# Two seams of the gated MLP and the first loads of a two-layer decoder trunk, rearranged together

## The chip, the cores and the metric

The kernel runs on one core of one Trainium2 chip. The metric is the device time of one execution in microseconds (us), given as the median of three runs. All stretches below are counted from the start of the profiled span.

## The reference, cut to what matters

Two layers over 1024 positions of width 1024, in float32. The first has a differential attention and causal pooling beside each other, the second a sliding-window attention; each ends in the same gated MLP.

```python
def conv_glu_ffn(x, norm_g, w_up, conv_w, conv_b, w_down):
    S = x.shape[1]
    h = rms_norm(x, norm_g) @ w_up                      # 1024 -> 2 x 2816
    hp = jnp.pad(h, ((0, 0), (CONV_W - 1, 0), (0, 0)))
    c = conv_b
    for j in range(CONV_W):
        c = c + conv_w[j] * hp[:, j:j + S]
    gate, up = jnp.split(c, 2, axis=-1)
    return x + (jax.nn.silu(gate) * up) @ w_down        # 2816 -> 1024

def reference(x, ...):
    for layer in range(DEPTH):                          # DEPTH = 2
        x = diff_pool_layer(x, ...) if layer % 2 == 0 else swa_layer(x, ...)
        x = conv_glu_ffn(x, f_norm[layer], f_w_up[layer], ...)
    return x
```

## The kernel before, in words

Everything is held transposed: the model's width lies on the 128 partitions (eight tiles `x[d]`), the 1024 positions on the free axis, in two halves of 512 columns. Each float32 operand is split into a high part (ScalarE copy, L131) and a low part (VectorE subtraction, L132), and each product of two operands is three matmuls (high by high, high by low, low by high). The tile framework's scheduler fixes the order of each engine's instructions when the kernel is built, by priorities (`urgent`) and a model of time; on the chip each engine runs its list in that order and waits on semaphores. So a late instruction holds up all that stand behind it on its engine, or on its DMA queue.

In order of time the program does: loads, RMS norm and the pooling projections (`run`, `a_pools`, 0 to 53 us); mixer A (to 400); `ffn_up` of layer 0 (416 to 864); `ffn_down` of layer 0 (to about 1045); mixer C (to 1450); `ffn_up` and `ffn_down` of layer 1 (1452 to 2122).

**The beginning.** `run` issues everything on SyncE's queue: the parameters, then by turns two tiles of the first half of x (L997) and one 512 KB pooling weight `a_u[i]` (L152, `load_split`), which is split in one piece of 1024 columns. `a_pools` (L945) goes through d for two weights together.

**The start of ffn_up.** `scaled_feed` gets each finished tile of x (h is its half), squares it on ScalarE into an `hf` tile (a pool of four buffers) and sums the squares on VectorE; after the last, `norm_stats` transposes the sum on TensorE (L240), computes 1/sqrt on VectorE, broadcasts it with TensorE (L251), and VectorE scales the eight tiles (L341), which are split. The first three of 22 pairs of weight tiles are multiplied plainly (`plain`, L372): i = 0 and 1 on the first half, i = 0 and 1 on the second, then i = 2. Each product is 24 matmuls and ends in an evacuation by ScalarE (L411). The evacuated tiles go through the convolution (ScalarE L379, VectorE L380 and L382) and the gate (L388, L392). The rest is done by seven products per i; their operands are sums of weight tiles, VectorE L466.

**The start of ffn_down.** Seven products p = 1, 5, 6, 3, 7, 2, 4, each over K = 11 chunks k of 12 matmuls (L634). For product 1, chunk k needs a weight tile and the tile `b11[k]` of the gated activations, for product 5 the sums of two of each. `fetch` loads weights on SyncE's queue into a pool that `stages` names (L571, or L578 for two halves), FETCH chunks ahead; `gather` makes the sums LEAD chunks ahead (VectorE L592), `prepare` splits the operands AHEAD chunks ahead. The activations come back from DRAM (`gd`) on GpSimd's queue: `b1` (k below EARLY, four tiles), `b11` from k = 4 (L673), `b11` below 4 (L676), `b12` (L677), x (L680), `b22` (L682), `b21` (L684). The last gated tile is stored to `gd` shortly before.

Of the kernel before, what the change touches and what calls it, by code (L numbers as in the profile page):

```python
# [13 lines left out]
F32 = mybir.dt.float32  # L14
F32R = mybir.dt.float32r
I32 = mybir.dt.int32
AF = mybir.ActivationFunctionType
# [38 lines left out]
LO_OUT = 0  # L56
EARLY = 4
AHEAD = 3
LEAD = 8
FETCH = 14  # L60

PAR_NORM = 0
PAR_AQ, PAR_AK, PAR_SUB, PAR_CQ, PAR_CK = 32, 33, 34, 35, 36
# [5 lines left out]
class Trunk:  # L69
# [251 lines left out]
    def scaled_feed(self, x):  # L321
        nc = self.nc

        def after(d, h, xs):
            with self.urgent(8000):
                if d is not None:
                    nc.scalar.dma_start(self.nspill[d * P:(d + 1) * P, h * HALF:(h + 1) * HALF], xs)
                    sq = self.half()
                    nc.scalar.activation(sq[:], xs, AF.Square)
                    if d == 0:  # L330
                        self.nacc[h] = sq
                    else:
                        acc = self.nacc[h]
                        nc.vector.tensor_tensor(out=acc[:], in0=acc[:], in1=sq[:], op=ALU.add)
                    return
                self.norm_stats(h)
                sl = slice(h * HALF, (h + 1) * HALF)
                for k in range(ND):
                    g = self.par[:, PAR_NORM + 8 * self.nidx + k:PAR_NORM + 8 * self.nidx + k + 1]
                    xs = x[k][:, sl]  # L340
                    nc.vector.scalar_tensor_tensor(  # L341
                        out=xs, in0=xs, scalar=g, in1=self.nrbc[:, sl], op0=ALU.mult, op1=ALU.mult)
                    self.split2(xs, self.nxg[k][h])
        return after

    def ffn_up(self, layer, x, gd):
# [72 lines left out]
        plain(1, 0, 0, "s", "T")  # L419
        plain(1, 0, 1, "q", "T")  # L420
        raws[2] = load(2, ("wr", "wr"))
        plain(0, 1, 0, "s", "T")
        plain(0, 1, 1, "q", "T")
        weights(2)
        plain(1, 1, 0, "s", "T")
        plain(1, 1, 1, "q", "T")


        T1, T2, T3, T4 = [], [], [], []
# [117 lines left out]
    def ffn_down(self, layer, xs, gd, after, begin=lambda part: None):  # L547
# [7 lines left out]
        pairs = {1: (0, lo), 6: (0, lo), 3: (K, lo), 2: (K, lo), 4: (K, hi)}  # L555
        raws, parts, ops = {}, {}, {}
        stages = {p: ("r", "wr", "r", "wr", "r") for p in (5, 6, 3, 7, 2)}
        stages[1], stages[4] = ("wr", "wr", "x", "x", "x", "x"), ("r",)
        taken = dict.fromkeys(stages, 0)

        def stage(p):
# [33 lines left out]
        def operand(src):  # L595
            op = self.big("ws", F32R, HL)
            self.split2(src, op)
            return op
# [23 lines left out]
        def prepare(p, k):  # L622
            l, m = parts.pop((p, k))
            with self.urgent(12000):
                ops[p, k] = operand(l), operand(m)

        banks = {}

# [40 lines left out]

        for n in range(FETCH):  # L670
            fetch(*seq[n])
        for k in range(EARLY, K):
            nc.gpsimd.dma_start(b11[k], g(k, hi))  # L673
        for k in range(K):
            if k < EARLY:
                nc.gpsimd.dma_start(b11[k], g(k, hi))  # L676
            nc.gpsimd.dma_start(b12[k], g(k, lo))  # L677
        x = [self.big("x") for _ in range(ND)]
        for d in range(ND):
            nc.gpsimd.dma_start(x[d][:], xs[d * P:(d + 1) * P, :])  # L680
        for k in range(K):
            nc.gpsimd.dma_start(b22[k], g(K + k, lo))  # L682
        for k in range(K):
            nc.gpsimd.dma_start(b21[k], g(K + k, hi))  # L684
        for n in range(LEAD):
            gather(*seq[n])
        for n in range(AHEAD):
# [615 lines left out]
    def run(self):  # L1303
# [8 lines left out]
        self.nc.sync.dma_start(self.par[:], I["params"])  # L1312
        x = [self.big("x") for _ in range(ND)]
        w = []
        for i in range(4):
            self.load_half(I["xT"], x, 0, 2 * i, 2 * i + 2)
            w.append(self.load_split(I["a_u"][i], eng=self.nc.vector, stage="wr" if i < 2 else "t"))
        self.idn = self.pc.tile([P, P], F32, name="idn", tag="idn")
        self.nc.sync.dma_start(self.idn[:], I["ident"])
        self.load_half(I["xT"], x, 1, 0, ND)  # L1320
# [123 lines left out]
```

## Time and profile before

| | |
|---|---|
| median of 3 runs | 2121.87 us (2121.12 to 2127.75) |
| the profiled execution | 2124.41 us, its span 2122.2 us |
| TensorE busy | 2016.3 us (95%) in 10440 matmuls |
| VectorE, ScalarE, GpSimd busy | 1602.0 us (75%), 1107.2 us (52%), 257.8 us (12%) |
| the chain that ended last | TensorE 82%, VectorE 7%, ScalarE 4%, DMA 3% |
| mean granted clock of TensorE | 0.982 |

TensorE is the engine whose work fills the span; what is not its work is the time in which it stands idle and the stretches in which its granted clock is below 1. The page averages over stages with different limits, so the argument is made from single stretches. Besides TensorE's list of waits, the timelines of the two seams of each MLP and of the first 14 us are what is to be read.

### The profile page before, as it was taken

How to read it: one execution, taken by the hardware profiler on the slowest of the kernel's cores; microseconds unless marked ns; L12 is line 12 of the kernel's file. 1: busy time of each engine (PE TensorE's matmuls, PEld its weight loads, DVE VectorE, ACT ScalarE, POOL GpSimd, SP SyncE). 2: the span in 40 equal slices, each digit the busy share in tenths (PEclk: the TensorE clock that was granted, in tenths of full speed). 3: DMA queues.
4: the chain of work that ended last, by engine and by line, in shares of the span. 5: the costliest groups of instructions: out<-in, count | busy, mean ns of one | idle time of the engine just before them, and what ended most of it. 6: DMA issues, size and time to landing. Idle time of an engine off the chain costs nothing.

```text
span 2122.2 us, 28436 instructions
## 1 busy us (share of the span) xinstructions
PE 2016.3 (95%) x10440; PEld 1719.0 (81%) x10440; DVE 1602.0 (75%) x2882; ACT 1107.2 (52%) x2115; POOL 257.8 (12%) x449
## 2 busy tenths in 40 slices
PE   8999999889999999699999989999999999979999
PEld 6999877677888888588789988777788888867887
DVE  6677787877787777598863887777978777758975
ACT  5476755444455554345454875654645455433443
POOL 0322452000000002300013321200000000031000
PEclk9999999999999999899999999999999999999999
DMA  4210121302212224763431101212221222268342
GB/s 170 90 49 23 64 95 61 119 30 90 90 70 86 84 90 164 275 217 105 144 115 40 51 21 50 73 58 80 92 87 70 80 90 90 89 229 312 100 164 85
DMA packets 82333, 216.97 MB, mean 102 GB/s; under 512 B 9361, under 2 KB 9873, under 8 KB 82193
## 3 DMA queue, kind: packets, MB, share of 16 engines
q1 hardware_dynamic: 65296, 169.00, 23.0%
q0 software_dynamic: 9984, 33.56, 4.3%
q10 hardware_dynamic: 6912, 12.59, 1.6%
q8 instruction: 82, 1.34, 0.3%
q14 instruction: 59, 0.48, 0.1%
HBM read 173.17 MB, written 41.94 MB: 101 GB/s over the span
## 4 chain that ended last, share of the span: by engine, by line
PE 82%; DVE 7%; ACT 4%; DMA 3%; issue 2%; POOL 1%; SPq 0%; ACTq 0%; DVEq 0%; POOLq 0%
PE pss L372 22%; PE psq L372 12%; PE pss L634 7%; PE psq L634 6%; PE psd L720 6%; PE psd L123 5%; PE psd L372 5%; PE psd L634 4%; PE pss L720 3%; PE psq L123 2%; PE psq L893 1%; DMA b<-gd 1%; PE pss L945 1%; PE pss L791 1%; PE pss L792 1%
## 5 line engine op out<-in xcount | busy, mean ns | idle before, releaser
L372 PE MATMUL pss<-xg,ws 128*128 128x512 f32 x1248 | 297.0, 391 | 10.8 <-DVE xg L132 6.1
L372 PEld LDWEIGHTS pss<-xg,ws 128*128 128x128 f32 x1248 | 234.5, 189 | 62.3 <-DVE xg L132 7.0
L634 PE MATMUL pss<-ws,ws 128*128 128x512 f32 x726 | 209.5, 398 | 34.3 <-ACT ws L131 27.0
L372 PE MATMUL pss<-T,ws 128*128 128x512 f32 x912 | 224.6, 390 | 3.4 <-ACT ws L131 3.4
L372 PEld LDWEIGHTS pss<-T,ws 128*128 128x128 f32 x912 | 171.1, 188 | 39.6 <-ACT ws L131 4.2
L634 PEld LDWEIGHTS pss<-ws,ws 128*128 128x128 f32 x726 | 138.0, 192 | 66.1 <-ACT ws L131 27.9
L634 PE MATMUL psq<-ws,ws 128*128 128x512 f32 x660 | 191.5, 393 | 0.0
L720 PE MATMUL psd<-ws,xg 128*128 128x256 f32 x1344 | 184.0, 285 | 2.2 <-DVE hms L729 1.7
L720 PEld LDWEIGHTS psd<-ws,xg 128*128 128x128 f32 x1344 | 171.5, 191 | 4.7 <-DVE hms L729 2.3
L372 PE MATMUL psq<-xg,ws 128*128 128x512 f32 x696 | 168.5, 391 | 0.0
L132 DVE TENSOR_TENSOR ws<-hf,ws 128x512 fp32r<-128x512 f32 x160 | 109.6, 689 | 73.4 <-ACT ws L131 73.1
L372 PEld LDWEIGHTS psq<-xg,ws 128*128 128x128 f32 x696 | 131.1, 188 | 27.2
L131 ACT ACTIVATE ws<-wr 128x512 fp32r<-128x512 f32 (+1 forms) x156 | 114.2, 737 | 68.9 <-PE pss L372 23.7
L634 PEld LDWEIGHTS psq<-ws,ws 128*128 128x128 f32 x660 | 125.4, 190 | 26.4
L634 PE MATMUL psd<-ws,ws 128*128 128x512 f32 x462 | 145.6, 397 | 0.8 <-DVE ms L242 0.8
L123 PE MATMUL psd<-xg,ws 128*128 128x512 f32 x528 | 140.2, 404 | 3.1 <-DVE x L272 2.3
L131 ACT ACTIVATE ws<-hf 128x512 fp32r<-128x512 f32 x160 | 100.0, 630 | 76.1 <-PE psq L372 33.3
L677 POOL DMA_DIRECT2D xg<-gd x22 | 12.1, 552 | 988.8 <-PE pss L372 961.0
L132 POOL TENSOR_TENSOR ws<-wr,ws 128x1024 fp32r<-128x1024 f32 x38 | 95.0, 2506 | 284.8 <-ACT ws L131 242.3
L380 DVE SCALAR_TENSOR_TENSOR x<-x,conv,x 128x1023 f32<-128x1023 f32 x80 | 102.6, 1282 | 29.2 <-ACT x L379 28.9
L123 PEld LDWEIGHTS psd<-xg,ws 128*128 128x128 f32 x528 | 97.1, 192 | 23.2 <-DVE x L272 4.3
L372 PE MATMUL psq<-T,ws 128*128 128x512 f32 x456 | 115.6, 390 | 0.0
(263 smaller groups left out, 4071.1 us busy)
## 6 DMA issues: line engine op xcount, KB each, us to landing
wr<-in_dram SPq DMA_DIRECT2D x102, 512.0 KB, 3.5
x<-in_dram SPq DMA_DIRECT2D x44, 512.0 KB, 4.4
gd<-x SPq DMA_DIRECT2D x40, 512.0 KB, 2.6
r<-in_dram SPq DMA_DIRECT2D x64, 256.0 KB, 3.8
r<-in_dram SPq DMA_DIRECT2D x28, 512.0 KB, 3.8
xd<-x ACTq DMA_DIRECT2D x48, 256.0 KB, 2.2
xg<-gd POOLq DMA_DIRECT2D x44, 256.0 KB, 5.2
b<-gd POOLq DMA_DIRECT2D x44, 256.0 KB, 8.6
```

Source lines behind the costliest of these rows:

```text
L123: self.nc.tensor.matmul(out, a, b, start=(k == 0), stop=(k == n - 1))
L131: nc.scalar.activation(hi, raw, AF.Copy)
L132: (eng or nc.vector).tensor_tensor(out=lo, in0=raw, in1=hi.bitcast(F32), op=ALU.subtract)
L372: nc.tensor.matmul(bank[:], a, b, start=start and k == 0, stop=k == n - 1, skip_group_check=open)
L380: nc.vector.scalar_tensor_tensor(out=c[:, 1:], in0=hr[:, :S - 1], scalar=cw(1), in1=c[:, 1:], op0=ALU.mult, op1=ALU.add)
L634: nc.tensor.matmul(banks[p][m][:], l, r, start=opens and n == 0, stop=closes and n == 2, skip_group_check=p != 2)
L677: nc.gpsimd.dma_start(b12[k], g(k, lo))
L720: self.nc.tensor.matmul(out, a, m[:, d % 4, :], start=(n == 0), stop=(n == 23))
L791: nc.tensor.matmul(out, q[:, qs], his[m][:, ks], start=True, stop=False)
L792: nc.tensor.matmul(out, q[rows, qs], lo[rows, ks], start=False, stop=True)
L893: nc.tensor.matmul(po[:, :256], tt[:, kb * P:(kb + 1) * P], v, start=(b == 0 and t == 0), stop=(b == j and t == 1))
L945: nc.tensor.matmul(pu[:], a, b, start=d + n == 0, stop=d == ND - 1 and n == 2)
```

## The change

Three parts. `scaled_feed` squares the tiles of the second half into the pool `t` in place of `hf`, and the four second-half products of i = 0 and 1 run as four open banks, chunk by chunk, with their four evacuations behind them. In `ffn_down` the weights of product 1 are staged in `wr` alone and those of product 5 in `r, r, wr`; LEAD and FETCH are smaller; `b12` and eight `b22` are issued first, and `b11` below 4, x, the last three `b22` and `b21` are issued later: each such load is preceded by a one-column ScalarE copy into its tile out of the operand of a given chunk, so that it can't start before this chunk is prepared. At the beginning ScalarE's queue issues the first half of x, and the pooling weights are loaded and split by halves, two tensors by turns.

```diff
-LEAD = 8
-FETCH = 14
+LEAD = 5
+FETCH = 11
...
-                    sq = self.half()
+                    sq = self.half() if h == 0 else self.big("t", F32, (P, HALF))
...
-        plain(0, 1, 0, "s", "T")
-        plain(0, 1, 1, "q", "T")
+        four = [(i, k, self.bank(b)) for i in range(2) for k, b in ((0, "s"), (1, "q"))]
+        for kh in range(2):
+            for d in range(4):
+                for i, k, po in four:
...
+                    for n, (a, b) in enumerate(((ah, bh), (ah, bl), (al, bh))):
+                        nc.tensor.matmul(po[:], a, b, start=kh + d + n == 0, stop=kh * d * n == 6)
         weights(2)
-        plain(1, 1, 0, "s", "T")
-        plain(1, 1, 1, "q", "T")
+        for i, k, po in four:
+            nc.scalar.activation(hrs[i, k][:, h1], po[:], AF.Copy)
...
-        stages[1], stages[4] = ("wr", "wr", "x", "x", "x", "x"), ("r",)
+        stages[1], stages[5], stages[4] = ("wr",), ("r", "r", "wr"), ("r",)
...
                 ops[p, k] = operand(l), operand(m)
+            release(p, k)
...
+        x = [self.big("x") for _ in range(ND)]
+        asked = {}
+        def ask(dst, src, when):
+            asked.setdefault(when, []).append((dst, src))
+        def release(p, k):
+            for dst, src in asked.pop((p, k), ()):
+                nc.scalar.activation(dst[:, 0:1], ops[p, k][0][:, 0, 0:1].bitcast(F32), AF.Copy)
+                nc.gpsimd.dma_start(dst, src)
         for k in range(EARLY, K):
             nc.gpsimd.dma_start(b11[k], g(k, hi))
         for k in range(K):
-            if k < EARLY:
-                nc.gpsimd.dma_start(b11[k], g(k, hi))
             nc.gpsimd.dma_start(b12[k], g(k, lo))
-        x = [self.big("x") for _ in range(ND)]
+        for k in range(K - 3):
+            nc.gpsimd.dma_start(b22[k], g(K + k, lo))
+        for k in range(EARLY):
+            ask(b11[k], g(k, hi), (1, 4))
         for d in range(ND):
-            nc.gpsimd.dma_start(x[d][:], xs[d * P:(d + 1) * P, :])
+            ask(x[d][:], xs[d * P:(d + 1) * P, :], (1, 5 + d) if d < 4 else (5, d - 3))
+        for k in range(K - 3, K):
+            ask(b22[k], g(K + k, lo), (5, k - 2))
         for k in range(K):
-            nc.gpsimd.dma_start(b22[k], g(K + k, lo))
-        for k in range(K):
-            nc.gpsimd.dma_start(b21[k], g(K + k, hi))
+            ask(b21[k], g(K + k, hi), (6, k))
...
-        for i in range(4):
-            self.load_half(I["xT"], x, 0, 2 * i, 2 * i + 2)
-            w.append(self.load_split(I["a_u"][i], eng=self.nc.vector, stage="wr" if i < 2 else "t"))
+        for d in range(ND):
+            self.nc.scalar.dma_start(x[d][:, :HALF], I["xT"][d * P:(d + 1) * P, :HALF])
+        for two in ((0, 1), (2, 3)):
+            raws = [self.big("wr" if i < 2 else "t") for i in two]
+            pairs = [(self.big("ws", F32R), self.big("ws", F32R)) for _ in two]
+            for sl in (slice(0, HALF), slice(HALF, S)):
+                for i, raw in zip(two, raws):
+                    self.nc.sync.dma_start(raw[:, sl], I["a_u"][i][:, sl])
+            for sl in (slice(0, HALF), slice(HALF, S)):
+                for raw, (wh, wl) in zip(raws, pairs):
+                    with self.urgent():
+                        self.split(raw[:, sl], wh[:, sl], wl[:, sl])
+            w += pairs
```

What stands where in the engines' lists, at the two places that carry most: first SyncE's queue at the start of ffn_down of layer 0. `wr` at L571 (before) and L577 (after) is a pair of product 1's weight tiles, `x` at L571 too; `wr` and `r` at L578 or L584 are product 5's. Before:

```order
L571 DMA wr_8220<-in_dram 128x2x512
L393 DMA gd_72<-x_7915 128x1024
L578 DMA wr_8233<-in_dram 128x512 x2
L578 DMA wr_8333<-in_dram 128x512 x2
L393 DMA gd_72<-x_8054 128x1024
L578 DMA wr_8396<-in_dram 128x512 x2
L578 DMA r_8230<-in_dram 128x512
L571 DMA x_8222<-in_dram 128x2x512
L571 DMA x_8224<-in_dram 128x2x512
```

And with the change:

```order
L577 DMA wr_8232<-in_dram 128x2x512
L393 DMA gd_72<-x_7927 128x1024
L577 DMA wr_8234<-in_dram 128x2x512
L577 DMA wr_8236<-in_dram 128x2x512
L393 DMA gd_72<-x_8066 128x1024
L584 DMA r_8310<-in_dram 128x512 x2
L584 DMA r_8331<-in_dram 128x512 x2
L584 DMA r_8383<-in_dram 128x512 x2
L584 DMA r_8406<-in_dram 128x512 x2
L351 DMA conv_14370<-in_dram 128x176
L577 DMA wr_8238<-in_dram 128x2x512
```

The weights of chunks 4 to 7 (before `x_8222` and `x_8224`, behind six loads for product 5; now `wr_8234` and `wr_8236`) stand ahead of product 5's and ahead of the store of the last gated tile but one, and those of chunks 8 and 9 (`wr_8238`) behind four loads for product 5.

Second, TensorE's list at the start of ffn_up of layer 0. L372 with `pss` and `psq` are products of the first half up to L251, L429 those of the second half. Before:

```order
L372 MATMUL pss_5084<-xg_4524,ws_5048 128x512 x2
L240 MATMUL psd_4936<-idn,hf_4870 128x128 x4
L372 MATMUL pss_5084<-xg_4524,ws_5048 128x512
L372 MATMUL pss_5084<-xg_4526,ws_5048 128x512 x3
L372 MATMUL psq_5111<-xg_4512,ws_5051 128x512 x3
...
L372 MATMUL psq_5111<-xg_4526,ws_5051 128x512 x3
L251 MATMUL psd_4962<-idn,r_4528 128x128 x4
```

And with the change:

```order
L372 MATMUL pss_5069<-xg_4538,ws_5027 128x512 x3
L240 MATMUL psd_4948<-idn,t_4882 128x128 x4
L372 MATMUL pss_5096<-xg_4524,ws_5057 128x512 x2
L251 MATMUL psd_4974<-idn,r_4540 128x128 x4
L372 MATMUL pss_5096<-xg_4524,ws_5057 128x512
L372 MATMUL pss_5096<-xg_4526,ws_5057 128x512 x3
```

The transposes (L240) moved ahead by 20 matmuls, from behind 68 of the first half to behind 48; of the 28 that stood between them and the broadcast (L251), two are left there, and 46 follow it. In layer 1 the transposes keep their place behind 37 matmuls, and 11 in place of 35 stand between them and the broadcast. On ScalarE all four evacuations of the second half stand behind its last matmul; before, two stood ahead of it.

## Rows read from the trace of the kernel before

**Rows 1.** TensorE's waits: engine, line, releaser: us in total, times, longest.

```profile
PE pss L634 <- ACT ws L131: 27.0, 2, 13.5
PE pss L634 <- DVE ws L132: 7.3, 5, 2.9
```

**Rows 2.** Windows: length, busy (x) of PE, PEld, DVE, ACT, POOL; PEclk, DMA share, GB/s.

```profile
462.19:499.75 37.56, 36.06 (x160) 29.52 (x158) 30.90 (x38) 25.26 (x38) 0.00 (x0) 1.00 0.28 98
864.00:884.00 20.00, 6.51 (x28) 5.11 (x27) 8.11 (x8) 5.78 (x8) 11.72 (x22) 0.77 0.87 308
912.00:960.00 48.00, 48.00 (x213) 39.77 (x212) 47.82 (x80) 19.46 (x35) 0.00 (x0) 1.00 0.50 172
```

**Rows 3.** Timeline of TensorE, ffn_down of layer 0: start, us, what [idle before <-releaser].

```profile
866.63 2.88 PE L372 MATMUL psq<-xg,ws 128*128 128x512 f32 x12
869.35 0.61 PE L634 MATMUL psd<-ws,ws 128*128 128x512 f32 x2
883.46 1.22 PE L634 MATMUL pss<-ws,ws 128*128 128x512 f32 x2 [13.49 <-ACT ws L131]
...
895.11 1.95 PE L634 MATMUL pss<-ws,ws 128*128 128x512 f32 x4 [2.69 <-DVE ws L132]
...
909.73 0.84 PE L634 MATMUL psd<-ws,ws 128*128 128x512 f32 x3
```

**Rows 4.** Timelines of ScalarE, SyncE's queue, GpSimd and VectorE in that gap.

```profile
881.31 0.63 ACT L131 ACTIVATE ws<-x 128x512 fp32r<-128x512 f32 x1 [9.41 <-DMA x<-in_dram]
...
868.87 3.14 SPq L571 DMA_DIRECT2D x<-in_dram  x4
...
867.69 2.65 POOL L673 DMA_DIRECT2D b<-gd  x5
...
873.26 1.28 DVE L382 SCALAR_TENSOR_TENSOR x<-x,conv,x 128x1022 f32<-128x1022 f32 x1
```

**Rows 5.** DMA issues from 864 to 884 us: KB each, median us to landing.

```profile
b<-gd POOLq DMA_DIRECT2D x15, 256.0 KB, 8.3
x<-in_dram SPq DMA_DIRECT2D x3, 512.0 KB, 15.6
xg<-gd POOLq DMA_DIRECT2D x5, 256.0 KB, 4.5
```

**Rows 6.** Timeline of TensorE, ffn_down of layer 1.

```profile
1911.35 1.22 PE L634 MATMUL pss<-ws,ws 128*128 128x512 f32 x2 [13.52 <-ACT ws L131]
```

**Rows 7.** Timelines of VectorE and TensorE, ffn_up of layer 0.

```profile
425.12 3.08 DVE L334 TENSOR_TENSOR hf<-hf,hf 128x512 f32<-128x512 f32 x4 [0.46 <-ACT T L411]
...
432.69 0.60 PE L240 MATMUL psd<-idn,hf 128*128 128x128 f32 x4
...
436.11 0.16 DVE L173 SCALAR_TENSOR_TENSOR r<-ntv,nyv 128x4 f32<-128x4 f32 x1
...
439.51 1.05 PE L251 MATMUL psd<-idn,r 128*128 128x128 f32 x8
...
448.48 1.65 PE L372 MATMUL pss<-xg,ws 128*128 128x512 f32 x3 [4.59 <-DVE xg L132]
...
470.89 5.60 PE L372 MATMUL pss<-xg,ws 128*128 128x512 f32 x24
...
499.95 0.73 PE L372 MATMUL pss<-T,ws 128*128 128x512 f32 x2 [1.70 <-ACT ws L131]
```

**Rows 8.** Timeline of TensorE, ffn_up of layer 1.

```profile
1498.75 5.60 PE L372 MATMUL pss<-xg,ws 128*128 128x512 f32 x24
...
1527.81 0.73 PE L372 MATMUL pss<-T,ws 128*128 128x512 f32 x2 [1.70 <-ACT ws L131]
```

**Rows 9.** Timeline of the first 10 us, ScalarE and TensorE.

```profile
4.21 0.72 ACT L224 ACTIVATE xg<-x,par 128x512 fp32r<-128x512 f32 x1 [1.98 <-DMA x<-in_dram]
...
8.06 1.06 ACT L131 ACTIVATE ws<-wr 128x1024 fp32r<-128x1024 f32 x1 [1.48 <-DMA wr<-in_dram]
...
9.17 5.04 PE L945 MATMUL pss<-xg,ws 128*128 128x512 f32 x10 [9.17 <-ACT ws L131]
```

More of the change, by code (lines that the diff above doesn't have):

```diff
@@ L421, in ffn_up @@
         raws[2] = load(2, ("wr", "wr"))
-        plain(0, 1, 0, "s", "T")
-        plain(0, 1, 1, "q", "T")
+        four = [(i, k, self.bank(b)) for i in range(2) for k, b in ((0, "s"), (1, "q"))]
+        for kh in range(2):
+            for d in range(4):
+                for i, k, po in four:
+                    ah, al = (ops[i][k][kh][:, t, d * P:(d + 1) * P] for t in range(2))
+                    bh, bl = (B[kh][1][d][:, t, :] for t in range(2))
+                    for n, (a, b) in enumerate(((ah, bh), (ah, bl), (al, bh))):
+                        nc.tensor.matmul(po[:], a, b, start=kh + d + n == 0, stop=kh * d * n == 6)
         weights(2)
-        plain(1, 1, 0, "s", "T")
-        plain(1, 1, 1, "q", "T")
+        for i, k, po in four:
+            nc.scalar.activation(hrs[i, k][:, h1], po[:], AF.Copy)
         T1, T2, T3, T4 = [], [], [], []
```

## The prediction

> **What bounds the kernel now.** TensorE is busy for 95% of the span, so time can only be won where it stands idle or runs at half its clock. I read its list of waits first. The longest entry is one kind of wait, product matmuls of ffn_down (L634) on a ScalarE split: 27.0 us in only two waits; a further 7.3 us go to VectorE splits of the same products [rows 1]. In the window 864 to 884 us TensorE is busy for 6.51 of 20 us while the DMA engines are 0.87 busy at 308 GB/s [rows 2]: the seam between the two halves of the MLP is a burst of loads.
>
> The timeline shows the seam of layer 0. TensorE ends the fourth chunk of product 1 at about 870.0 and restarts at 883.46, 13.49 us later; it loses 2.69 us more before 895.11, and product 1 ends at 909.73 + 3 x 0.227 = 910.4 [rows 3]. (A matmul takes 0.227 us: 12 of them from 866.63 to 869.35.) Between 883.46 and 892.42 stand 28 matmuls, which would be 6.35 us at this rate: that is the lower of the clock's two levels (1.2 and 2.4 GHz), and it costs 2.6 us; the mean granted clock was 0.77 of full in the idle window, 1.00 from 912 us on [rows 2, 3]. Layer 1 has the same gap, 13.52 us [rows 6].
>
> What ends the gap is a weight. ScalarE's split at 881.31 had waited for the DMA of `x<-in_dram`, which SyncE issued at 868.87 [rows 4]. Such loads took 15.6 us from issue to landing in this window, while GpSimd pushed `b` tiles beside them, at 8.3 us each [rows 5]. The convolution of the last gated tile had been over at 873.26 + 1.28 = 874.5 [rows 4].
>
> **The change, part by part: ffn_down.** The weights of chunks 4 to 7 get `wr` buffers and stand before product 5's on SyncE's queue, ahead of the last stores. The 12.4 us from 868.87 to the split at 881.31 go with them. Late next is `b11[4]`. GpSimd issued its first `b` at 867.69 behind five `xg`, and 2.65 us for five is 0.53 each; three stand ahead now, so about 866.6. Its landing is between the medians of `xg` and `b` in the burst, 4.5 and 8.3 us: 871.1 to 874.9 [rows 4, 5]. I take 5.5 us (872.1), since the nearly 2 MB of `x<-in_dram` that shared the engines are gone. Then VectorE's list decides: the low part of `b11[4]` stands behind the convolution that ends at 874.5 [rows 4], so the steady flow begins at about 875.2. From there: seven chunks of 12 matmuls, 84 x 0.227 = 19.0; half clock after a shorter idle stretch, taken as 1.4 (half of the 2.6 shown; ends 0 and 2.6); 0.9 for the gate's product, which VectorE does ahead of chunk 5's low part (one 1024-column operation and sums, some 4 us of its list against 2.72 of TensorE). Product 1 ends at 896.5 in place of 910.4: -13.9.
>
> Given back: at the end of product 1 VectorE adds four banks to x and has seven sums and splits in its list up to the low part of (5, 2). A VectorE operation of 512 columns takes about 0.6 us in a row, 47.82 / 80 in the packed window [rows 2], so 11 x 0.6 = 6.6 us against the 24 matmuls (5.4 us) of (5, 0) and (5, 1): 1.2 us idle. That is -12.7 a layer, **-25.5** for two.
>
> The 26 one-column copies a layer go to ScalarE, which is busy for 19.46 of 48 us while product 5 runs [rows 2]: nothing, unless a claimed tile is not free. The deferred loads (`b11` below 4, x, `b21`) are needed chunks later; TensorE's work covers them. If VectorE, at 47.82 of 48 us [rows 2], were behind for good, it would cost. But its list from 875 to the end of product 6 adds up to about 14 + 44 + 44 splits and sums, 8 bank additions and a dozen for product 3, 122 x 0.6 = 73 us, against 19.0 + 22 x 2.72 = 79 us of matmuls. The cover is thin, and LEAD 5 leaves fewer sums done ahead.
>
> **ffn_up.** In layer 0 the transposes came at 432.69 behind 68 matmuls, though the sum of squares had been complete since 425.12 + 3.08 = 428.2 [rows 7]. Behind 48 they can start at 428.2. From the transposes at 432.69 to `r` at 436.27 VectorE took 3.6 us [rows 7]; only two matmuls cover it now, so TensorE idles about 3 us, until 432, where the broadcast came at 439.51 before. The operands are then ready 7.5 us earlier, and the 4.59 us wait before 448.48 is gone [rows 7]: 46 matmuls to 443.3, 96 to 465.1, in place of 470.89. That is -5.8 for this piece. But the four evacuations now stand behind its end. From the first convolution on VectorE (462.19) to the sums that feed product 6 (499.75), VectorE was busy for 30.90 of 37.56 us [rows 2]; about 2.4 of that were weight splits that can be done sooner. Evacuation and ScalarE's first convolution step are a half and a whole width, 0.5 and 1.1 us by the split of [rows 9], so at best 465.1 + 1.6 + 28.5 = 495.2, with no idle gap at all; with a third of the old 6.7 us of gaps, about 497.5. Product 6 started at 499.95 [rows 7]: -2.5. In layer 1 the second half ended at 1498.75 and product 6 began 29.06 us later [rows 8]; the four-bank piece has no idle of that size to lose, ends at about 1498, and the same chain gives 1498 + 32.4 = 1530.4 against 1527.81: +2.5. TensorE will be idle 4 to 5 us before product 6 in both; half clock after that, as after the 4.59 us of [rows 7], is bounded by 0 and 2.6 each; I take 0.5. Sum **+1** (ends -4 and +7).
>
> **The beginning.** The first tile of x had landed at 4.21, the first 512 KB weight at 8.06, and TensorE began at 9.17, after a split of 1.06 us [rows 9]. Half a weight is as large as the tile of x and is issued where that one was; sharing the engines with x it lands at about 5. ScalarE's list then has a copy and a square of x (0.7 each), one DMA issue (nearest row: GpSimd's 0.53) and half a split (0.5) before the first matmul: 4.21 + 0.7 + 0.7 + 0.5 + 0.5 = 6.6, or -2.6. More such issues lie in ScalarE's list among the operations that feed TensorE, so I take **-2** (ends 0 and -2.6).
>
> The Trainium skill speaks against this part ("Trainium Kernel Development and Optimization", Key Constraints): loads issued by SyncE, ScalarE and GpSimd all run on the same 16 DMA engines and interleave, and several issuers save issue time only. By that rule x on ScalarE's queue wins nothing, and the change would win 2 us less. The 15.6 and 8.3 us of [rows 5] show, with it, that loads hinder each other. I stay with -2 because it rests on the smaller first weight load, not on the second queue.
>
> **Sum.** -25.5 + 1 - 2 = -26.5. The profiled execution took 2124.41, so 2097.9; the median of the runs lies 2.5 below it: **2095**.
>
> **The rivals.**
> 1. *The burst of loads still binds.* If `b` tiles land after 8.3 us and later ones keep arriving a chunk late, restart is 877.5, half clock 2.6, further stalls 3.2 as before: 877.5 + 19.0 + 2.6 + 3.2 = 902.3, and (5, 2) still waits: -7 a layer, 2107. For it: 0.87 DMA share [rows 2]. Against: nearly 2 MB of weights are out of the burst. 0.20.
> 2. *ffn_up pays for late evacuations.* Gaps on VectorE stay, and half clock follows both idle stretches: +7 there, 2101. For it: 30.90 of 37.56 us [rows 2]; against: ScalarE has room. 0.14.
> 3. *The deferred loads stop VectorE: slower.* Four sums that need `b11` below 4 stand in VectorE's list ahead of chunk (1, 10). They are asked for at about 875.2, four issues are 2.1 us, and 8.3 us to landing give 885.6 [rows 5]; (1, 10) is needed at 893.8. It decides from a landing at about 892; every us after that is one of TensorE's, in both layers. To end 0.3% slower it must eat 33 us, a landing at about 908; at 910 the time is 2132. For it: 15.6 us was seen in this window [rows 5], and the loads queue behind eleven others. Against: the burst is over by then. 0.05.
> 4. *The second queue wins nothing at the start*, nor does the half load, since x takes the bandwidth: 2097. The 15.6 us of [rows 5] speak for it, the landing at 8.06 of a load twice as large [rows 9] against. 0.10. The rule of the Trainium skill cited above says it of the queue.
>
> **How the numbers follow.** The forecast has 0.51. About 0.3%, 6.4 us, is what a measurement can tell from no change. Forecast, 2 and 4 are faster (0.75); of rival 1 I count 0.12 as faster and 0.08 as within 0.3%; rival 3 is slower. Faster 0.87, same 0.08, slower 0.05. Range: with all terms at their better ends the seams give at most 13.5 + 2.6 + 3 = 19 a layer (2079 with the rest at its better ends, too good to count); rival 1 with ffn_up at +7 is 2113. I take 2082 to 2112.
>
> **What would show it.** Right: after the fourth chunk of product 1 an idle stretch of 3 to 6 us that a VectorE or ScalarE split of `b` ends, product 1 over some 14 us sooner after it began, no `x<-in_dram` there; broadcasts of ffn_up behind a wait of about 3 us in layer 0, and a wait of 4 to 6 us before product 6; a first matmul at 6 to 7 us. Wrong: an idle stretch of over 8 us at the seam, waits in product 5 on sums or on their weights, or a VectorE that stands still for GpSimd's loads.

## The result and the profile after

The changed kernel takes 2109.7 us (median of 4 runs, 2108.17 to 2111.8) against 2122.52; the ratio is 0.9939, 95% interval 0.9924 to 0.9953. That is 0.6% faster and within the range, but 13 us and not 27. The profiled execution took 2108.35 us with a span of 2106.6, 15.6 less than before.

Where it went, by the length of TensorE's stages in the two traces (from the first or last matmul of one stage to that of the next, in us):

| stage | before | after | difference | forecast |
|---|---|---|---|---|
| first matmul | 9.17 | 6.38 | -2.8 | -2 |
| to the start of ffn_up, layer 0 | 407.8 | 412.8 | +4.9 | 0 |
| ffn_up, layer 0 | 452.5 | 452.6 | +0.1 | -2 |
| ffn_down, layer 0 | 232.1 | 222.9 | -9.2 | -12.7 |
| mixer C | 350.3 | 349.5 | -0.9 | 0 |
| ffn_up, layer 1 | 445.4 | 446.9 | +1.5 | +3 |
| ffn_down, layer 1 | 220.8 | 211.6 | -9.1 | -12.7 |

So two terms failed: the seam of ffn_down gave 9 in place of 12.7 in each layer, and what the beginning won was gone again when ffn_up began, with 2 us more. These are single traces; how far the stretch to ffn_up differs between executions of the same lists is told in the last section.

First the waits of TensorE in the changed kernel (engine, line, releaser: us in total, times, longest). L641 is the product of ffn_down, L964 the pooling projection. (p, k) stands for chunk k of product p; four of its twelve matmuls need only high parts, the eight behind them a low part too:

```profile
PE pss L372 <- ACT ws L131: 10.8, 4, 4.3
PE pss L641 <- DVE ws L132: 9.2, 7, 2.5
PE pss L641 <- ACT ws L131: 6.7, 3, 3.4
...
PE pss L964 <- ACT ws L131: 6.4, 1, 6.4
```

Against [rows 1], the ScalarE wait of the products fell from 27.0 to 6.7, while their VectorE wait rose from 7.3 to 9.2, and ffn_up's wait for ScalarE splits is new at the top.

The seam of ffn_down in layer 0, TensorE's timeline (start, us, what, idle before it and what ended that):

```profile
871.62 0.61 PE L641 MATMUL psd<-ws,ws 128*128 128x512 f32 x2
875.60 0.74 PE L641 MATMUL pss<-ws,ws 128*128 128x512 f32 x2 [3.37 <-ACT ws L131]
...
877.93 2.07 PE L641 MATMUL pss<-ws,ws 128*128 128x512 f32 x4 [1.12 <-DVE ws L132]
...
884.77 2.08 PE L641 MATMUL pss<-ws,ws 128*128 128x512 f32 x4 [2.50 <-DVE ws L132]
...
910.09 0.73 PE L641 MATMUL pss<-ws,ws 128*128 128x512 f32 x2 [1.18 <-DVE ws L132]
```

The gap of 13.49 us [rows 3] is 3.37 and 1.12 now. But at chunk 5 there is one of 2.50 (before, one of 2.69 stood at chunk 6), and the 8 matmuls behind it take 3.25 us, 0.41 each: the lower clock level again, as in the 8 behind the wait of 1.12. VectorE, ScalarE and SyncE's queue say what chunk 5 waited for:

```profile
872.21 0.68 DVE L502 TENSOR_TENSOR x<-snap,psq 128x512 f32<-128x512 f32 x1
...
877.80 0.68 DVE L132 TENSOR_TENSOR ws<-wr,ws 128x512 fp32r<-128x512 f32 x1
881.68 0.69 DVE L598 TENSOR_TENSOR xg<-r 128x512 f32<-128x512 f32 x1 [3.20 <-DMA r<-in_dram]
882.29 0.68 DVE L598 TENSOR_TENSOR b<-xg,b 128x512 f32<-128x512 f32 x1
882.89 1.22 DVE L392 TENSOR_TENSOR x<-x,x 128x1024 f32<-128x1024 f32 x1
884.03 0.69 DVE L132 TENSOR_TENSOR ws<-b,ws 128x512 fp32r<-128x512 f32 x1
...
872.92 1.51 SPq L584 DMA_DIRECT2D r<-in_dram  x3
```

VectorE stood still for 3.20 us on a sum for product 5, whose weight SyncE issued at 872.92. The low part of chunk 5's `b` (884.03) is behind that sum in VectorE's list, and TensorE behind it. SyncE had issued the weight of (5, 0) ten microseconds sooner; this one it could issue only once VectorE had read the last `snap` tile of ffn_up (872.21 + 0.68 = 872.89), and SyncE's list of waits has 9.1 us there for L502: ffn_down's pool lies in the memory that ffn_up's pool had, and the second and third `r` buffer lie where the `snap` tiles were.

The start of ffn_up in layer 0, TensorE, SyncE's queue and ScalarE:

```profile
430.45 0.60 PE L240 MATMUL psd<-idn,t 128*128 128x128 f32 x4
435.38 1.22 PE L372 MATMUL pss<-xg,ws 128*128 128x512 f32 x2 [4.33 <-ACT ws L131]
436.40 1.91 PE L251 MATMUL psd<-idn,r 128*128 128x128 f32 x8
...
471.42 5.60 PE L372 MATMUL pss<-xg,ws 128*128 128x512 f32 x24
...
501.86 1.22 PE L372 MATMUL pss<-T,ws 128*128 128x512 f32 x2 [3.07 <-ACT ws L131]
...
431.08 0.80 SPq L357 DMA_DIRECT2D T<-in_dram  x2
...
434.70 2.42 ACT L131 ACTIVATE ws<-T 128x512 fp32r<-128x512 f32 x4 [3.45 <-DMA T<-in_dram]
```

The transposes moved ahead as the list said. But the wait behind them is 4.33 us, and not for `r`: it is for the weights of i = 1, which SyncE loads into `T` at 431.08, when the sum of squares in `t` has been transposed (its wait ends with L240; in the kernel before it issued this load at 393.18). Again a pool of the next stage lies where the last one's tiles are read last. Product 6 began 82.7 us after ffn_up's start, against 82.9 [rows 7].

The third place is mixer A, in which no line was changed. VectorE's timeline, and TensorE's:

```profile
96.44 2.36 DVE L768 TENSOR_TENSOR x<-x,hr 128x1024 f32<-128x1024 f32 x2 [3.20 <-POOL x L1023]
98.72 0.17 DVE L989 TENSOR_TENSOR t<-t,cnt 128x15 f32<-128x15 f32 x1
...
101.29 0.74 PE L123 MATMUL psq<-g,hf 128*128 128x512 f32 x2 [2.00 <-ACT g L131]
101.87 1.80 PE L739 MATMUL pss<-ws,xg 128*128 128x256 f32 x10
```

Two products of the head norms (L768) wait for GpSimd and hold up the last pooling window (L989), which needs nothing of them; before, the window stood ahead of them in VectorE's list. TensorE's lead of 4.4 us at 48.5 us (52.88 to 48.52, the first matmuls of L720, L739 now) is down to 0.5 at the first head transposes (110.72 to 110.20).

### The profile page after: what moved, and what is told of

Its sections match the earlier page's. It is cut to its first block, busy times and chain, and to the rows that moved or that the text cites. A ratio compares the mean times of both kernels' runs of the same rounds, so it can differ in the third digit from the quotient of the medians.

```text
span 2106.6 us, 28572 instructions
## 1 busy us (share of the span) xinstructions
PE 2021.0 (96%) x10440; PEld 1722.4 (82%) x10440; DVE 1604.1 (76%) x2886; ACT 1112.1 (53%) x2171; POOL 256.4 (12%) x449
## 4 chain that ended last, share of the span: by engine, by line
PE 79%; DVE 10%; ACT 6%; issue 2%; DMA 1%; POOL 1%; ACTq 0%; DVEq 0%; SPq 0%; POOLq 0%
PE pss L372 21%; PE psq L372 10%; PE pss L641 7%; PE psq L641 6%; PE psd L123 5%; PE psd L372 5%; PE psd L641 5%; PE psd L739 4%; PE pss L739 3%; PE psq L123 2%; PE psq L912 1%; PE pss L964 1%; PE psq L964 1%; PE pss L429 1%; PE pss L810 1%
## 5 line engine op out<-in xcount | busy, mean ns | idle before, releaser
L372 PE MATMUL pss<-xg,ws 128*128 128x512 f32 x1152 | 274.2, 392 | 6.6 <-ACT ws L131 4.6
L372 PEld LDWEIGHTS pss<-xg,ws 128*128 128x128 f32 x1152 | 217.4, 189 | 53.5 <-ACT ws L131 5.5
L372 PE MATMUL pss<-T,ws 128*128 128x512 f32 x912 | 227.0, 392 | 6.1 <-ACT ws L131 6.1
L641 PE MATMUL pss<-ws,ws 128*128 128x512 f32 x726 | 208.3, 397 | 15.9 <-DVE ws L132 9.2
L372 PEld LDWEIGHTS pss<-T,ws 128*128 128x128 f32 x912 | 172.7, 190 | 43.3 <-ACT ws L131 7.0
L641 PE MATMUL psq<-ws,ws 128*128 128x512 f32 x660 | 190.3, 393 | 0.0
L739 PE MATMUL psd<-ws,xg 128*128 128x256 f32 x1344 | 184.0, 284 | 2.2 <-DVE hms L748 1.7
L641 PEld LDWEIGHTS pss<-ws,ws 128*128 128x128 f32 x726 | 137.4, 191 | 48.7 <-DVE ws L132 12.5
L739 PEld LDWEIGHTS psd<-ws,xg 128*128 128x128 f32 x1344 | 171.4, 191 | 4.7 <-DVE hms L748 2.3
L131 ACT ACTIVATE ws<-wr 128x512 fp32r<-128x512 f32 (+1 forms) x172 | 123.3, 721 | 92.5 <-DMA wr<-in_dram 25.8
L641 PEld LDWEIGHTS psq<-ws,ws 128*128 128x128 f32 x660 | 125.3, 190 | 26.4
L641 PE MATMUL psd<-ws,ws 128*128 128x512 f32 x462 | 144.2, 396 | 0.8 <-DVE ms L242 0.8
L372 PE MATMUL psq<-xg,ws 128*128 128x512 f32 x600 | 143.3, 389 | 0.0
L372 PEld LDWEIGHTS psq<-xg,ws 128*128 128x128 f32 x600 | 112.6, 188 | 23.4
L132 DVE TENSOR_TENSOR ws<-wr,ws 128x512 fp32r<-128x512 f32 x134 | 91.6, 688 | 46.5 <-ACT ws L131 46.4
L372 PE MATMUL psq<-T,ws 128*128 128x512 f32 x456 | 115.6, 390 | 0.0
```

What stands on the lines that cost most here:

```text
L131: nc.scalar.activation(hi, raw, AF.Copy)
L132: (eng or nc.vector).tensor_tensor(out=lo, in0=raw, in1=hi.bitcast(F32), op=ALU.subtract)
L372: nc.tensor.matmul(bank[:], a, b, start=start and k == 0, stop=k == n - 1, skip_group_check=open)
L641: nc.tensor.matmul(banks[p][m][:], l, r, start=opens and n == 0, stop=closes and n == 2, skip_group_check=p != 2)
L739: self.nc.tensor.matmul(out, a, m[:, d % 4, :], start=(n == 0), stop=(n == 23))
```

## The experiments

Each kernel is compared with the kernel before, run beside it on the same chip, and given as its median, the ratio of the two and the ratio's 95% interval. The kernel before took 2122.97, 2121.89, 2121.21 and 2123.69 us (medians) in the four groups of runs.

### One part at a time

The hunks of the diff above by themselves. First those of the beginning:

```diff
-            self.load_half(I["xT"], x, 0, 2 * i, 2 * i + 2)
...
+            self.nc.scalar.dma_start(x[d][:, :HALF], I["xT"][d * P:(d + 1) * P, :HALF])
...
+                    self.nc.sync.dma_start(raw[:, sl], I["a_u"][i][:, sl])
```

> The kernel before with the third part alone (x issued by ScalarE, pooling weights by halves). Theory: the start is won (first matmul about 2.8 us sooner, the norm's end about 4 us sooner), but the scheduler's list for VectorE in mixer A is another one (two head-norm products that wait for GpSimd stand ahead of the last pooling window), which gives back about 6 us; ffn_up of layer 0 starts 2 us later than before, and the total is 2122.5 + 2 = 2124.5 (2122 to 2127). Rival: the start's gain stays (2118 to 2120), and what was lost in mixer A came with the pool of the first part.

Measured: 2129.92 us, ratio 1.0032 (1.0020 to 1.0045). The sign is that of the theory, the size is over it. The first matmul was at 6.58, and the same list as above stood on VectorE. The granted clock of these runs was lower, 0.981 in the median against 0.984 in the runs of the kernel before beside them. By an estimate from these two, 0.003 of 2123 us, that is 6.4 us, so nearly all of the loss may be clock.

Those of ffn_up:

```diff
+                    sq = self.half() if h == 0 else self.big("t", F32, (P, HALF))
...
+        four = [(i, k, self.bank(b)) for i in range(2) for k, b in ((0, "s"), (1, "q"))]
```

> The kernel before with the first part alone (squares in t, four open banks). Theory: mixer A as before; ffn_up takes about as long in layer 0 and 1.5 us longer in layer 1: 2124 (2122 to 2126). Rival: the pool t shared with mixer A delays mixer A, and the total is 2126 or more; other rival, the forecast's better end, 4 us won: 2118.

Measured: 2125.53 us, 1.0016 (1.0004 to 1.0028), as expected. In its trace, however, ffn_up of layer 1 is 4.9 us longer and not 1.5; why is open.

Those of ffn_down:

```diff
+LEAD = 5
+FETCH = 11
...
+        stages[1], stages[5], stages[4] = ("wr",), ("r", "r", "wr"), ("r",)
...
+            ask(b11[k], g(k, hi), (1, 4))
```

> The kernel before with the second part alone (the seam of ffn_down). Theory: 9.1 us won in each layer, 2122.5 - 18 = 2104 (2102 to 2107), with a stall of 2 to 3 us at chunk 5 of product 1 that a VectorE split ends, behind a sum that waited for a weight of product 5. Rival (the forecast): 12.7 us a layer, 2097.

Measured: 2108.7 us, 0.9938 (0.9920 to 0.9957), single runs from 2104.8 to 2115.1. In its trace ffn_down is 10.4 us shorter in layer 0 and 6.7 in layer 1, with waits at chunk 5 of 1.04 and 2.89 us. So the seam alone carries what the whole change brought (0.9938 against 0.9939); the forecast's 2097 is out.

The changed kernel with the beginning of the kernel before, so both of these parts:

```diff
+            self.load_half(I["xT"], x, 0, 2 * i, 2 * i + 2)
...
-            self.nc.scalar.dma_start(x[d][:, :HALF], I["xT"][d * P:(d + 1) * P, :HALF])
```

> The changed kernel without the third part. Theory: the third part costs about 2 us net, so 2105 to 2108, and mixer A ends when it did before. Rival: the third part pays, 2111 to 2114.

Measured: 2105.16 us, 0.9929 (0.9911 to 0.9947). The interval overlaps that of the whole change, so this run alone does not show that the third part costs; the run of the third part by itself shows it for that kernel.

### What chunk 5 waited for

The three `r` buffers are taken first, so that they lie where ffn_up's operands were, and the `b` buffers in reverse, so that the two that come to lie on the `snap` tiles are among the deferred ones:

```diff
+        rr = [self.big("r", F32, HL) for _ in range(3)]
-        bb = [self.big("b") for _ in range(K)]
+        bb = [self.big("b") for _ in range(K)][::-1]
```

> The changed kernel with the three r buffers of ffn_down taken first and the b buffers in reverse order, so that r lies where ffn_up's operands lay and the two deferred b tiles lie where its snap tiles lay. Theory: the second weight of product 5 was issued only when VectorE had read the last snap tile, and the stall of 2 to 2.5 us at chunk 5 of product 1 is its landing; here it is issued some 9 us sooner, the stall falls under 1 us and the half clock after it goes too: 2 to 3.5 us a layer, so 4 to 7 us under the changed kernel's 2109.7: 2103 to 2106. Rival: the stall is VectorE's own work (gate product and sums ahead of the low part), the burst makes the load late anyway, and the time stays: 2108 to 2111.

Measured: 2105.63 us, 0.9915 (0.9901 to 0.9928). The stall at chunk 5 is gone in both layers. VectorE, ScalarE and TensorE of this kernel:

```profile
874.41 0.68 DVE L599 TENSOR_TENSOR xg<-r 128x512 f32<-128x512 f32 x1
...
876.75 0.68 DVE L132 TENSOR_TENSOR ws<-b,ws 128x512 fp32r<-128x512 f32 x1
...
885.89 0.63 ACT L131 ACTIVATE ws<-wr 128x512 fp32r<-128x512 f32 x1 [8.27 <-DMA wr<-in_dram]
...
887.09 0.73 PE L642 MATMUL pss<-ws,ws 128*128 128x512 f32 x2 [0.91 <-ACT ws L131]
```

The sum waits for nothing now. In this trace SyncE issues the second weight of product 5 at 859.78 without a wait, and it has landed at 866.0. The edit moves no instruction: on every engine the order in this trace is that of the changed kernel's, so only the places of the buffers differ, and with them the stall went. New waits for weights stand further on: 0.91 us at chunk 8 here, 3.06 at chunk 10 in layer 1.

The time tells less than the stall. The interval overlaps that of the changed kernel, and in the traces ffn_down is 2.8 us shorter in layer 0 and 1.2 longer in layer 1. The rest of the 8.3 us between the two spans lies in mixers A and C (3.8 and 2.7), whose lists are the same.

The same edit on the kernel with the hunks of ffn_down alone:

> The second part alone, with the same order of the r and b buffers. Theory: what the run of the second part alone took (median 2108.7, most runs near 2105) less 4 to 7: 2099 to 2104, the fastest so far. Rival: as that run, 2105 to 2109.

Measured: 2105.66 us, 0.9924 (0.9908 to 0.9940): a miss. The stall at chunk 5 went here too (no wait there in either layer), but waits of 2.58 us at chunk 10 and 2.35 in product 5 took its place in layer 1, and ffn_down is as long as without the edit (221.6 and 214.6 us against 221.7 and 214.0). Here too the order on every engine is the same in both traces.

The loads at the seam of layer 0 with the `r` buffers first, from 866 to 890 us (KB each, median us to landing):

```profile
x<-xd POOLq DMA_DIRECT2D x4, 512.0 KB, 9.0
...
wr<-in_dram SPq DMA_DIRECT2D x1, 512.0 KB, 11.3
```

Four loads of x, which are not needed before product 1 ends, go beside the weight of chunk 8. So they were asked for later:

```diff
-            ask(x[d][:], ..., (1, 5 + d) if d < 4 else (5, d - 3))
+            ask(x[d][:], ..., (1, 8 + d // 2) if d < 4 else (5, d - 3))
```

> The changed kernel with the r buffers first, and the first four tiles of x asked for at chunks 8 and 9 of product 1 in place of 5 to 8. Theory: the new wait for the weights of chunk 8 (0.9 us in layer 0, 3.1 in layer 1) comes from three 512 KB loads of x beside them in the burst and goes; 2 to 4 us under the run with the r buffers first (2105.6): 2102 to 2104. Rival: SyncE's queue and the other loads make those weights late, or x now comes late for the additions to the banks after product 1, 2105 to 2110.

Measured: 2101.21 us, 0.9899 (0.9881 to 0.9916). The weight of chunk 8 lands in 9.5 us:

```profile
wr<-in_dram SPq DMA_DIRECT2D x1, 512.0 KB, 9.5
```

Chunks 8 and 10 wait for weights no longer in either layer (0.19 us for a VectorE split is left at chunk 10 in layer 0), and ffn_down takes 219.4 and 208.4 us. x came in time: VectorE waits for nothing in the additions after product 1. Before (5, 2) stand 1.77 us, in layer 0 in place of 0.78 and 1.17. The interval of the total overlaps that of the run with the `r` buffers first; the same edit is told apart below, on the kernel that also has x of the beginning on SyncE's queue.

### The two halves of the first part

The squares in `t` alone:

```diff
-                    sq = self.half()
+                    sq = self.half() if h == 0 else self.big("t", F32, (P, HALF))
```

> The kernel before with the squares of the second half in the pool t, and nothing else. Theory: this alone reorders mixer A from 245 to 309 us and costs 2.5 us there; the transposes of ffn_up move ahead, which wins nothing by the time product 6 begins: 2124 to 2127. Rival: the four open banks reorder mixer A, and this kernel runs as before, 2121 to 2124.

Measured: 2120.98 us, 0.9993 (0.9982 to 1.0004): the theory was wrong, this kernel runs as before, and up to 410 us its order of instructions is that of the kernel before on every engine. Its transposes of ffn_up moved ahead, and the wait behind them is that of the changed kernel, for a load that was issued late (SyncE's queue and TensorE):

```profile
431.64 0.80 SPq L357 DMA_DIRECT2D T<-in_dram  x2
...
435.86 1.22 PE L372 MATMUL pss<-xg,ws 128*128 128x512 f32 x2 [4.25 <-ACT ws L131]
```

The four open banks alone, which is the other hunk of ffn_up:

```diff
-        plain(0, 1, 0, "s", "T")
...
+        for i, k, po in four:
+            nc.scalar.activation(hrs[i, k][:, h1], po[:], AF.Copy)
```

> The kernel before with the four open banks alone, squares as before. Theory: mixer A as before; the evacuations behind the last matmul cost 0 to 3 us before product 6 in each layer: 2123 to 2127. Rival: nothing is lost, since VectorE and ScalarE have room: 2121 to 2123.

Measured: 2133.2 us, 1.0042 (1.0029 to 1.0054), worse than expected. Product 6 waits longer, as in the changed kernel:

```profile
502.12 0.73 PE L372 MATMUL pss<-T,ws 128*128 128x512 f32 x2 [3.07 <-ACT ws L131]
```

It was 1.70 us before [rows 7]. ffn_up is 2.5 and 2.3 us longer in its trace. ffn_down of layer 0 is 4.4 us longer too; why is open. The granted clock of these runs was 0.9785 in the median against 0.984 beside them; by the same kind of estimate, 0.0055 of 2122 us, that is 11.7 us, as much as the whole loss. With the squares in `t` as well, in the run of the first part, the whole part cost only 3 us, so the two hunks do not add up.

### The beginning

x back on SyncE's queue, by turns with the half weights:

```diff
-        for d in range(ND):
-            self.nc.scalar.dma_start(x[d][:, :HALF], ...)
...
+            for h, sl in enumerate((slice(0, HALF), slice(HALF, S))):
+                self.load_half(I["xT"], x, 0, 2 * two[0] + 2 * h, 2 * two[0] + 2 * h + 2)
```

> The changed kernel with the first half of x back on SyncE's queue, by turns with the half weights. In its list for VectorE the last pooling window stands ahead of the two head-norm products again. Theory: the half weight brings the early start without ScalarE's queue (first matmul at 6.5 to 7.5 us), and the stretch to the first head transposes takes 57.8 us as in the kernel before in place of 61.7, so 3 to 4 us under the changed kernel: 2105 to 2107. Rival: the second queue brings the start (first matmul at 8 us or later here), and the total is 2108 to 2111.

Measured: 2106.14 us, 0.9920 (0.9906 to 0.9934). The first matmul is at 7.08 us, and from the dense projection's first matmul to the first head transposes 57.2 us pass, where the changed kernel took 61.7 (48.52 to 110.20). The two stretches as windows, in this order (length, busy us of TensorE and the others, granted clock, DMA share, GB/s):

```profile
50.32:107.52 57.20, 57.20 (x433) 55.06 (x432) 38.03 (x41) 24.11 (x51) 20.35 (x25) 1.00 0.23 84
```

```profile
48.52:110.20 61.68, 59.69 (x442) 57.28 (x440) 35.98 (x41) 24.85 (x51) 18.80 (x25) 0.97 0.25 84
```

Part of that is clock: the run with the `r` buffers first, with the changed kernel's lists, took 60.1 at a granted clock of 1.00. And the total, though as expected, is not clear of the changed kernel's (0.9939) nor of that of the run without the third part (0.9929).

The other way round, x on ScalarE's queue and the weights whole:

```diff
-        for two in ((0, 1), (2, 3)):
...
+        for i in range(4):
+            w.append(self.load_split(I["a_u"][i], eng=self.nc.vector, stage="wr" if i < 2 else "t"))
```

> The changed kernel with x on ScalarE's queue, but the pooling weights loaded and split whole. The head-norm products stand ahead of the last pooling window here. Theory: first matmul no sooner than 7.5 us, and 60 to 62 us to the first head transposes: as the changed kernel or up to 3 us slower, 2109 to 2114. Rival: the queue alone brings the start, 2107 to 2109.

Measured: 2109.87 us, 0.9945 (0.9932 to 0.9959); first matmul at 7.35, a little sooner than expected, then 61.7 us in that stretch.

Whether the list is what costs is told best by the third part alone with the one queue or the other. This is the edit of the run with x on SyncE's queue, made on the kernel before with the hunks of the beginning:

> The kernel before with the third part alone, but x on SyncE's queue by turns with the half weights; the last pooling window stands ahead of the head-norm products in VectorE's list. Theory: the loss of the run with the third part alone (2129.9) came from that list, and this kernel is 5 to 9 us faster than that one: 2119 to 2123, no slower than the kernel before. Rival: the list in mixer A is not what costs, the half weights or something after mixer A do, and this kernel takes 2126 or more.

Measured: 2117.52 us, 0.9972 (0.9961 to 0.9983), 12 us under the run of the third part alone and 6 under the kernel before. VectorE and TensorE of the kernel with ScalarE's queue:

```profile
97.21 2.36 DVE L749 TENSOR_TENSOR x<-x,hr 128x1024 f32<-128x1024 f32 x2 [3.20 <-POOL x L1004]
99.48 0.17 DVE L970 TENSOR_TENSOR t<-t,cnt 128x15 f32<-128x15 f32 x1
...
102.06 0.73 PE L123 MATMUL psq<-g,hf 128*128 128x512 f32 x2 [2.02 <-ACT g L131]
```

And with SyncE's:

```profile
93.49 0.17 DVE L970 TENSOR_TENSOR t<-t,cnt 128x15 f32<-128x15 f32 x1
...
99.14 2.36 DVE L749 TENSOR_TENSOR x<-x,hr 128x1024 f32<-128x1024 f32 x2 [1.84 <-POOL x L1004]
...
96.09 0.73 PE L123 MATMUL psq<-g,hf 128*128 128x512 f32 x2
```

The window is done 6 us sooner, and TensorE doesn't wait. That accounts for some 1.8 us at the first head transposes (109.40 and 107.64); the rest of the 12 arises later, in mixers A and C, where the two traces part again (421.0 and 412.3 us at the start of ffn_up; the stretch from 244 to 311 us took 67.3 us in the first, from 242 to 306 us 63.8 in the second).

Behind the first head transposes, in mixer A, it is not the order. From there up to 410 us the two kernels, and the kernel before, have the same order of instructions on every engine. To the start of ffn_up they need 311.6 and 304.6 us, with TensorE idle for 17.9 and 16.7 of them, at a granted clock of 0.96 and 0.99; the kernel before 306.3, 17.7 and 0.98. So most of the difference there is clock. The other kernels go the same way: 304.6 to 307.1 us in the five traces with half weights and x on SyncE's queue, 306.2 to 309.0 in the seven with the old beginning, 306.5 to 311.9 in the five with x on ScalarE's queue. Why the clock is lower behind one beginning than behind the other stays open.

### All mends together

Two of them, the `r` buffers first and x on SyncE's queue, on the changed kernel:

> The changed kernel with both: r buffers first, and x on SyncE's queue with half weights. Theory: the two gains add, 2109.7 - 4 - 3 to 4: 2101 to 2103, the fastest. Rival: other moves in the lists of mixer A and C take one of them back, 2104 to 2107.

Measured: 2100.96 us, 0.9903 (0.9890 to 0.9917), as expected.

With the later x as well, which is the only difference to the run just told:

> All three mends on the changed kernel: r buffers first, x asked for at chunks 8 and 9, x of the beginning on SyncE's queue. Theory: each was worth 4 us by itself (2105.6, 2101.2 after 2105.6, 2106.1), 2109.7 - 12 = 2097 to 2100. Rival: they overlap or the lists of mixer C take some back, 2100 to 2104.

Measured: 2095.24 us, 0.9865 (0.9849 to 0.9881), a little better than expected, and its interval is clear of the run without the later x. What is left of the products' waits in ffn_down:

```profile
PE pss L642 <- ACT ws L131: 5.7, 2, 2.9
PE pss L642 <- DVE ws L132: 5.4, 5, 1.6
```

And without the hunks of ffn_up:

> The same without the first part (ffn_up as in the kernel before). Theory: the first part is worth nothing in layer 0 and costs 1.5 us in layer 1, so as the run with all three mends or up to 2 us under it. Rival: the first part pays in the list of mixer C (its stretch was 2 us shorter in several runs with it), 2 to 4 us over that run.

Measured: 2093.61 us, 0.9851 (0.9834 to 0.9867), the fastest kernel, 1.5% under the one before; its interval overlaps that of the one with the first part, so that part is worth nothing that these runs can tell.

## Why the prediction was right and wrong

**The seam of ffn_down: mechanism right, one term mis-sized.** The weights left the path, `b11[4]` became the next thing, and the low part behind the convolution set the steady flow, as forecast: it begins at 877.9 on this trace's own time. The forecast's 875.2 plus the 2.3 us by which the stage began later is 877.5, 0.4 apart. The gap gave 9 us of its 13.5. The step that failed is "0.9 for the gate's product, which VectorE does ahead of chunk 5's low part". It counted VectorE's own work and took the sums for ready; the weights that they need had no term. One sum waited 3.20 us for a weight, so the stall was 2.50, with half clock behind it (8 x 0.18 = 1.4 us more) besides the 1.4 that the forecast has for chunk 4. The two runs with the `r` buffers first show the cause: without that wait there is no stall at chunk 5.

Product 1 took 29.4 us from the end of chunk 3 (901.64 - 872.23) in place of 26.5, before 40.4. The forecast also counted 84 matmuls from 875.2 on; four of them had run in the gap, so 80 were left, 0.9 us less. The idle of product 5 was forecast at 1.2 us and measured at 0.48 + 1.18. That is -11.0 + 1.7 = -9.3, close to the measured -9.2. With the `r` buffers first and x asked for later ffn_down takes 219.3 and 207.8 us in the run with all mends, 12.8 and 13.0 less than before: the forecast's 12.7 comes out once the two kinds of late weight that it had not seen are gone.

**ffn_up: the sum about right, by other steps.** Forecast +1, measured +1.6, which is luck. The idle stretch in layer 0 was forecast at 3 us, for `r`, and was 4.33, for a load that the `t` pool delays. The piece up to the second half's end won 1.6 and not 5.8: the broadcast came at 436.40 (forecast 432, here 434.1 with the later start), and half clock behind that wait, for which the piece had no term, held until about 440 us (granted clock 0.64 from 431.05). Product 6's start, forecast 2.5 us sooner, was 0.2 sooner. The rival with late evacuations named the right place: the wait before product 6 grew from 1.70 to 3.07.

**The beginning: the step was right, its reach was not.** The first matmul came 2.8 us sooner (forecast 2.6 at best), in part by luck: in the seven traces with the old beginning it is at 7.50 to 9.83 us, depending on when the first whole weight lands, 8.53 in the median, and in four with the changed one at 6.24 to 6.58, so about 2 us sooner. The step that failed is the one that added these 2 us to the sum as if nothing between there and the end could take them back. With the new beginning the scheduler, which works by a model of time, wrote another list for VectorE 90 us later, and the stretch behind it ran at a lower clock. By itself this part cost 7 us; with x on SyncE's queue it won 6. How much of these 13 us is the list, and what lowers the clock, is not shown.

The two kernels that split the third part start TensorE at 7.08 (half loads on one queue) and 6.38 us (on both). The 0.7 us between them is not a sooner landing: ScalarE reads the first tile of x at 4.14 us with one queue and at 4.52 with two. With one queue a square and a scaled copy more stand ahead of the first weight split in ScalarE's list, which begins at 6.42 in place of 5.70. As far as the first tile of x goes, that agrees with the rule of the Trainium skill ("Trainium Kernel Development and Optimization", Key Constraints) that several issuers share the same 16 DMA engines and save issue time only.

**The rivals.** That the burst still binds (rival 1) gave the nearest time, 2107, by luck and for another reason: `b11[4]` landed some 5.7 us after its issue (forecast 5.5, the rival 8.3), and the stall at chunk 5 was not for a `b`. Rival 3 (VectorE held up by deferred `b11`) did not occur: the sums with `b11` below 4 ran from 894.31 without a wait.

## What to carry to other kernels

Where one stage's pool is laid over the last one's, a load into it can't be issued before the last reader of the tile beneath is done; read from the lists of waits which buffer lies on what, and give the early loads the buffers that come free first. A gain at the start of a statically scheduled kernel is no gain until the later lists and the granted clock have been compared: the same half loads won 6 us or cost 7 with x on one queue or the other. The lists differ up to the first head transposes only, as far as mixer A goes; behind them the same lists ran at another clock. After a wait is removed, look for what waits behind the instruction that now comes first, on the same in-order list.

## What the runs showed of the hardware

The stretch of mixer A from 245 to 309 us took different times in kernels whose lists are the same up to there, on TensorE and the other engines. Two pairs, as windows (length, busy us of TensorE and the others, granted clock, DMA share, GB/s): the run with SyncE's queue and the same with the `r` buffers first, whose difference lies some 500 us later:

```profile
241.89:305.65 63.76, 57.25 (x338) 48.83 (x336) 49.43 (x119) 41.74 (x98) 35.03 (x60) 0.97 0.31 100
```

```profile
241.57:307.80 66.23, 58.85 (x337) 50.29 (x336) 51.30 (x119) 41.83 (x98) 34.74 (x60) 0.95 0.30 96
```

And the changed kernel beside the run with x asked for later:

```profile
244.88:311.02 66.14, 58.63 (x338) 50.19 (x336) 51.05 (x119) 41.72 (x98) 34.72 (x60) 0.95 0.29 96
```

```profile
244.05:311.45 67.40, 60.63 (x337) 52.24 (x336) 50.98 (x119) 41.82 (x98) 34.79 (x60) 0.90 0.29 95
```

In all of them TensorE stands idle for 6.5 to 7.5 us in short waits, and how long the lower clock level follows differs from execution to execution: 0.97 to 0.90 of full, 63.8 to 67.4 us. So a single trace can't tell a difference of 3 us in this stage, and the 2.5 us by which it was longer in the changed kernel's trace than before (66.1 against 63.6) may be of this kind; what the third part costs is told by the medians of many runs (9 and 10 of the two kernels with the third part alone).
